# Expert stage of a hybrid decoder block: down products in float32, norm factors on ScalarE, their product on VectorE

## The chip, the cores and the metric

The kernel runs on one core of a Trainium2 chip. A core has TensorE (matrix products, with a row of its own for weight loads), VectorE, ScalarE, GpSimd (POOL below) and SyncE (SP), which issues most DMAs; each engine takes its instructions in order. The metric is the device time in microseconds (us), as the median of three runs.

## What is computed

A decoder block for 2048 tokens of 1024 channels: an attention and pooling mixer, then a mixture of 32 experts of which each token takes two, then a final norm. The change touches the experts:

```python
def expert_block(args):
    xb, e = args
    return (jax.nn.silu(xb @ w_gate[e]) * (xb @ w_up[e])) @ w_down[e]

y_rows = lax.map(expert_block, (x_blocks, block_e)).reshape(R, D)
y_rows = y_rows * row_w[:, None].astype(y_rows.dtype)
out = jnp.zeros((T + 1, D), y_rows.dtype).at[row_token].add(y_rows)[:T]
...
return rmsnorm(x, norm_f_g)
```

All arrays are float32; `w_gate` and `w_up` are 1024 x 256 for each expert, `w_down` 256 x 1024.

## The kernel before

The mixer (four blocks of 512 tokens) comes first and ends with the routing, which writes tables of rows for each expert. Then the expert stage goes through 16 pairs of experts. An expert has 128 row slots; a pair has 56 more that its experts share (`RW`, `CAP`).

A product of float32 values is made of three products in f16 (`PASSES`): a value is split into a high half, its rounding to f16, and a low half, the rest. ScalarE writes the high half of a weight piece of 128x1024 (`msplit`, line 1170), VectorE the low half (line 1171). Weights are scaled by 64, which `DSC` takes out again.

The steps of a pair stand in `PLAN`, in the order in which they are handed to a scheduler, which then sets each engine's order by costs of its own:

- S: SP loads weight pieces (`mst` for gate and up, `msd` for down, 512 KB each, 12 a pair), and `msplit` splits those of the next pair into `mwh`.
- U (`mo_up`, line 1263): gate and up products of both experts, 192 matmuls of 184 columns.
- A (`mo_act`): sigmoid on ScalarE, two products on VectorE (lines 1272 and 1273) into `sg`, then the high half of the activations on ScalarE (line 1276) and the low half on POOL (line 1277), both in `ac`.
- X (`mo_x`): rows of the next pair, transposed by TensorE (line 1208; line 1221 for the shared ones, by selection products with `sel`), copied from PSUM to `xT` by ScalarE and VectorE (lines 1227 and 1229).
- R and B: gathers of rows (`mh`, line 1194) and of the sums so far (`mx`, line 1246), indirect DMAs that POOL issues.
- D (`mo_out`, line 1293): for each of the two experts two halves of 512 columns, 24 matmuls in all, which VectorE adds to `mx` (line 1296). For the shared rows (`mo_rest`, line 1306) 24 more, with either half of the columns on half of the array's columns, two at a time.
- F (`finish`): the square sum of a row on ScalarE (line 1337), its scaling on VectorE (1342), the power -0.5 on POOL (1343), times a flag on VectorE (1316). The norm factors y = gain x r + flag are made on VectorE (lines 1318 and 1322), the product of y and the sums on POOL (line 1323), and POOL stores it by an indirect DMA (line 1251).

The loads of the sums of a pair wait until the stores of the pair two before it have landed. Behind the last pair come two loops for rows past the capacity, which run zero times here.

## Time and profile before

| | |
|---|---|
| runs | 1747.66, 1753.17, 1753.48 us; median 1753.17 |
| span of the profiled execution, first to last instruction | 1743.5 us |
| the profiled execution's own time | not recorded apart; the runs lie 4 to 10 us above the span |
| TensorE busy | 1531.6 us (88%) |
| VectorE busy | 1231.3 us (71%) |
| POOL busy | 813.0 us (47%) |
| ScalarE busy | 706.3 us (41%) |
| mean granted clock of TensorE | 0.946 |

The granted clock is the share of TensorE's full clock (2.4 GHz) that it was given, between one half and one. A busy share over the whole span mixes stages with different limits, so a stage is read through windows of its own. The ends of matmuls are modelled, and records in a row overlap; the time from one start to the next tells what a matmul costs.

### The profile page before, as it was taken

What the parts mean: (1) busy time and instruction counts of PE and PEld (TensorE: products, weight loads), DVE (VectorE), ACT (ScalarE), POOL (GpSimd) and SP (SyncE); (2) the same over time, 40 slices, a digit from 0 to 9 for tenths busy, and PEclk for the clock granted to TensorE, in tenths of its full rate; (3) what the DMA queues carried; (4) which work ended last, traced back from release to release, by engine and by line L of the source; (5) the groups of instructions that cost most, each with busy time, mean ns of one, the idle gap of its engine ahead of it and who ended that gap; (6) DMA issues with size and microseconds to landing.
All of it is one profiled execution on the core that took longest, in us unless ns stands there. A gap on an engine that the chain in (4) does not pass through costs nothing.

```text
span 1743.5 us, 28315 instructions
## 1 busy us (share of the span) xinstructions
PE 1531.6 (88%) x10777; PEld 930.4 (53%) x10777; DVE 1231.3 (71%) x1941; ACT 706.3 (41%) x1089; POOL 813.0 (47%) x620
## 2 busy tenths in 40 slices
PE   6888989979999899999799999967897888888784
PEld 3364434447544347644347744446675676666563
DVE  7678886799737357736247743368898999998984
ACT  5633464533324231223230211234664565565541
POOL 1446453556324113423223401215777777777764
PEclk9999999989999999999999999977999899998997
DMA  7444689976859895658787557669688878878722
GB/s 251 133 128 156 218 251 245 285 235 248 268 164 220 274 326 195 187 161 223 193 262 227 163 167 206 172 227 333 222 299 281 295 258 302 305 260 285 264 89 77
DMA packets 244812, 394.70 MB, mean 226 GB/s; under 512 B 154507, under 2 KB 157963, under 8 KB 244672
## 3 DMA queue, kind: packets, MB, share of 16 engines
q1 hardware_dynamic: 222144, 324.50, 60.1%
q0 software_dynamic: 22528, 68.35, 10.7%
q8 instruction: 86, 1.41, 0.3%
q14 instruction: 54, 0.44, 0.1%
HBM read 294.03 MB, written 75.50 MB: 212 GB/s over the span
## 4 chain that ended last, share of the span: by engine, by line
PE 33%; issue 16%; DVE 14%; POOL 14%; DMA 9%; ACT 2%; SPq 1%; POOLq 0%; DVEq 0%; ACTq 0%
PE aux L321 6%; PE acc L321 5%; PE acc L751 5%; PE acc L504 4%; PE acc L736 4%; DMA bt<-bt 3%; DVE mwh L1171 2%; DVE w L173 2%; POOL y L1323 2%; PE acc L1293 2%; POOL out_dram L1251 2%; POOL mx L1246 2%; PE acc L1263 2%; DMA out_dram<-x 2%; DMA w<-in_wv_dram 2%
## 5 line engine op out<-in xcount | busy, mean ns | idle before, releaser
L1263 PE MATMUL acc<-xT,mwh 128*128 128x184 f16 x3072 | 247.6, 243 | 0.0
L1263 PEld LDWEIGHTS <-mwh 128*128 128x128 f16 x3072 | 243.8, 98 | 6.4 <-issue 6.3
L173 DVE SCALAR_TENSOR_TENSOR w<-w 128x1024 f16<-128x1024 f32 x110 | 158.2, 1445 | 93.4 <-ACT w L172 93.1
L1171 DVE SCALAR_TENSOR_TENSOR mwh<-mst,mwh 128x1024 f16<-128x1024 f32 x128 | 194.8, 1539 | 1.7 <-ACT mwh L1170 1.0
L751 PE MATMUL acc<-w,bt 128*128 128x512 f16 x768 | 171.5, 385 | 16.2 <-DMA bt<-bt 15.6
L736 PE MATMUL acc<-w,bt 128*128 128x512 f16 x768 | 170.9, 382 | 9.2 <-DVE et L330 6.5
L321 PEld LDWEIGHTS <-hS 128*128 128x128 f16 x1056 | 104.1, 100 | 135.4 <-issue 18.5
L172 ACT ACTIVATE w<-w 128x1024 f16<-128x1024 f32 x110 | 112.2, 1028 | 154.7 <-DMA w<-in_wv_dram 61.6
L1293 PE MATMUL acc<-mwh,ac 128*128 128x512 f16 x384 | 113.4, 445 | 54.2 <-POOL ac L1277 42.3
L1170 ACT ACTIVATE mwh<-mst 128x1024 f16<-128x1024 f32 x128 | 128.7, 1047 | 30.6 <-PE acc L1263 23.1
L1323 POOL TENSOR_TENSOR y<-mx,y 128x1024 f32<-128x1024 f32 (+1 forms) x45 | 112.5, 2500 | 51.6 <-DVE y L1318 37.7
L321 PE MATMUL aux<-w,hS 128*128 128x512 f16 x528 | 130.1, 397 | 6.5 <-ACT et L336 4.4
L751 PEld LDWEIGHTS <-bt 128*128 128x128 f16 x768 | 75.3, 99 | 111.5 <-DMA bt<-bt 17.1
L736 PEld LDWEIGHTS <-bt 128*128 128x128 f16 x768 | 75.2, 98 | 103.1 <-issue 13.8
L504 PEld LDWEIGHTS <-w 128*128 128x128 f16 x1176 | 112.1, 99 | 32.2 <-issue 7.1
L321 PEld LDWEIGHTS <-hT 128*128 128x128 f16 x792 | 77.2, 98 | 94.1 <-issue 2.7
L321 PE MATMUL acc<-w,hS 128*128 128x512 f16 x528 | 120.8, 379 | 1.6 <-DVE w L173 1.6
L741 POOL TENSOR_TENSOR et<-et 128x512 f32<-128x512 f32 x32 | 41.4, 1296 | 164.0 <-DVE et L739 164.0
L666 ACT ACTIVATE bt<-et 128x512 f16<-128x512 f32 x48 | 30.2, 629 | 196.2 <-POOL et L741 116.4
L330 DVE SCALAR_TENSOR_TENSOR et<-aux,et 128x512 f32<-128x512 f32 x99 | 65.7, 681 | 45.8 <-PE aux L321 45.8
L1293 PEld LDWEIGHTS <-ac 128*128 128x128 f16 x384 | 38.9, 111 | 110.3 <-POOL ac L1277 48.8
L380 POOL TENSOR_TENSOR w<-w 128x1024 f32<-128x1024 f32 x24 | 62.6, 2614 | 72.3 <-DVE w L173 29.7
(291 smaller groups left out, 2869.2 us busy)
## 6 DMA issues: line engine op xcount, KB each, us to landing
w<-wkeep SPq DMA_DIRECT2D x168, 512.0 KB, 4.7
mst<-in_we_dram SPq DMA_DIRECT2D x128, 512.0 KB, 6.8
wkeep<-w SPq DMA_DIRECT2D x70, 512.0 KB, 3.1
w<-in_wv_dram SPq DMA_DIRECT2D x64, 512.0 KB, 5.2
msd<-in_we_dram SPq DMA_DIRECT2D x64, 512.0 KB, 5.5
x<-in_x_dram SPq DMA_DIRECT2D x32, 512.0 KB, 5.3
w<-in_wm_dram SPq DMA_DIRECT2D x16, 512.0 KB, 4.9
out_dram<-x POOLq DMA_DIRECT2D x16, 512.0 KB, 6.4
```

The source lines that it names most:

```text
L172: nc.scalar.activation(w[:, 0, c:], f[:, c:], AF.Copy, scale=WSC)
L173: nc.vector.scalar_tensor_tensor(w[:, 1, c:], f[:, c:], WSC, w[:, 0, c:], op0=OP.mult, op1=OP.subtract)
L321: nc.tensor.matmul(p, L[name](i, c, k), w[k // 2][:, a, (k % 2) * 512:(k % 2 + 1) * 512], start=k == 0 and m == 0, stop=k == 3 and m == 2)
L330: nc.vector.scalar_tensor_tensor(o[i], ps[i], DSC, x[i], op0=OP.mult, op1=OP.add)
L504: nc.tensor.matmul(ps[:, :h], w[:, i, k * 128:(k + 1) * 128], L[name](c, k), start=k == 0 and m == 0, stop=k == 3 and m == 2)
L736: nc.tensor.matmul(ps, lhs, w[k // 2][:, a, (k % 2) * 512:(k % 2 + 1) * 512], start=k == 0 and i == 0, stop=k == 3 and i == 2)
L751: nc.tensor.matmul(ps, self.mT[t][k // 4][:, 4 * c + k % 4], w[hf][k // 2][:, a, (k % 2) * 512:(k % 2 + 1) * 512], start=k == 0 and i == 0 ...
L1170: nc.scalar.activation(w[:, 0], f, AF.Copy, scale=WSC)
L1171: nc.vector.scalar_tensor_tensor(w[:, 1], f, WSC, w[:, 0], op0=OP.mult, op1=OP.subtract)
L1263: nc.tensor.matmul(ps[:, c * CAP:(c + 1) * CAP], self.part(W[o], a, col, 128), xT[:, b, k], start=k == 0 and i == 0, stop=k == KT - 1 and ...
L1293: nc.tensor.matmul(ps, s["ac"][i][:, b, f, :128], self.part(s["W"][3 * i + 2], a, f * D + hf * 512, 512), start=f == 0 and n == 0, stop=f ...
L1323: (nc.vector if s["P"] == 15 else nc.gpsimd).tensor_tensor(y, x, y, op=OP.mult)
```

## The change

The down weights stay in float32 as they arrive: no split, no `mwh` for them, and 8 buffers `msd` instead of 4. The activations stay in float32 in `sg` (4 buffers instead of 2). The down products multiply these directly, one matmul instead of three. The scale of 16 x 64 in the weights of the rows goes. The norm factors move from VectorE to ScalarE, their product with the sums from POOL to VectorE. Comments and docstrings go too, so that the lines shift.

```diff
-        V.tensor_scalar(w, T[:, 1], DSC, None, op0=OP.mult)
+        V.tensor_copy(w, T[:, 1])
...
-        s["W"][i] = [self.msplit(f, self.mq if i % 3 == 2 else self.mw) for f in s["F"][i]]
+        s["W"][i] = s["F"][i] if i % 3 == 2 else [self.msplit(f, self.mw) for f in s["F"][i]]
...
-    BST, BSD = 8192 // PW, 4096 // PW
+    BST, BSD = 8192 // PW, 8192 // PW
...
-        sg = mp.tile([128, 2 * CAP], F32, name="sg", bufs=2)
+        sg = mp.tile([128, 2 * CAP], F32, name="sg", bufs=4)
         nc.scalar.activation(sg, pg, AF.Sigmoid, scale=DSC)
         nc.vector.scalar_tensor_tensor(sg, pg, DSC, sg, op0=OP.mult, op1=OP.mult)
-        nc.vector.scalar_tensor_tensor(sg, pu, DSC * ASC, sg, op0=OP.mult, op1=OP.mult)
-        ac = mp.tile([128, 2, 2, CAP], F16, name="ac", bufs=2)
-        sg3 = sg.rearrange("p (c t) -> p c t", c=2)
-        nc.scalar.activation(ac[:, 0], sg3, AF.Copy)
-        nc.gpsimd.tensor_tensor(ac[:, 1], sg3, ac[:, 0], op=OP.subtract)
-        s["ac"][h] = ac
+        nc.vector.scalar_tensor_tensor(sg, pu, DSC, sg, op0=OP.mult, op1=OP.mult)
+        s["ac"][h] = sg.rearrange("p (c t) -> p c t", c=2)
...
             for f in range(2):
-                for n, (a, b) in enumerate(self.PASSES):
-                    nc.tensor.matmul(ps, s["ac"][i][:, b, f, :128], self.part(s["W"][3 * i + 2], a, f * D + hf * 512, 512),
-                                     start=f == 0 and n == 0, stop=f == 1 and n == 2)
+                nc.tensor.matmul(ps, s["ac"][i][:, f, :128], self.part(s["W"][3 * i + 2], f * D + hf * 512, 512),
+                                 start=f == 0, stop=f == 1)
...
-        m = [(h, f, n) for h in range(2) for f in range(2) for n in range(3)]
-        for q, (h, f, n) in enumerate(m):
-            a, b = self.PASSES[n]
+        m = [(h, f) for h in range(2) for f in range(2)]
+        for q, (h, f) in enumerate(m):
             for hf in range(2):
-                nc.tensor.matmul(ps[hf * 64:(hf + 1) * 64], s["ac"][h][:, b, f, CAP - 64:],
-                                 self.part(s["W"][3 * h + 2], a, f * D + hf * 512, 512),
+                nc.tensor.matmul(ps[hf * 64:(hf + 1) * 64], s["ac"][h][:, f, CAP - 64:],
+                                 self.part(s["W"][3 * h + 2], f * D + hf * 512, 512),
                                  start=q == 0, stop=q == len(m) - 1, tile_position=(0, hf * 64))
...
         if i < 2:
-            nc.vector.tensor_scalar(y, self.gf, r, nl, op0=OP.mult, op1=OP.add)
+            nc.scalar.activation(y, self.gf, AF.Identity, bias=nl, scale=r)
         else:
             for h in range(2):
                 p = slice(h * 64, h * 64 + 64)
-                nc.vector.tensor_scalar(y[p], self.gf[p, h * 512:(h + 1) * 512], r[p], nl[p], op0=OP.mult, op1=OP.add)
-        (nc.vector if s["P"] == 15 else nc.gpsimd).tensor_tensor(y, x, y, op=OP.mult)
+                nc.scalar.activation(y[p], self.gf[p, h * 512:(h + 1) * 512], AF.Identity, bias=nl[p], scale=r[p])
+        nc.vector.tensor_tensor(y, x, y, op=OP.mult)
```

The scheduler makes new orders of it. Up to the routing the four compute engines issue the same rows. Two places in the middle of the expert stage follow, with the buffer numbers as they are.

ScalarE, one pair, before (`mwh` are splits, `sg` the sigmoid, `ac` the activations' high half, `y,fss` the square sum, `xT` the copies from PSUM):

```order
L1337 ACTIVATE y,fss<-mx_10459 128x1024
L1170 ACTIVATE mwh<-msd 128x1024 x4
L1337 ACTIVATE y,fss<-mx_10460 128x1024
L1170 ACTIVATE mwh<-mst 128x1024 x2
L1271 ACTIVATE sg<-acc 128x368
L1170 ACTIVATE mwh<-mst 128x1024 x2
L1276 ACTIVATE ac<-sg 128x368
L1337 ACTIVATE y,fss<-mx_10461 128x512
L1170 ACTIVATE mwh<-mst 128x1024 x2
L1271 ACTIVATE sg<-acc 128x368
L1170 ACTIVATE mwh<-mst 128x1024 x2
L1227 ACTIVATE xT<-auxh 128x8x128
```

The same stretch of ScalarE after the change:

```order
L1170 ACTIVATE mwh<-mst 128x1024 x2
L1228 ACTIVATE xT<-auxh 128x8x128 x2
L1332 ACTIVATE y,fss<-mx_10459 128x1024
L1313 ACTIVATE y<-gfr,tlm,frs 128x1024
L1228 ACTIVATE xT<-aux 128x4x2x56 x2
L1332 ACTIVATE y,fss<-mx_10460 128x1024
L1228 ACTIVATE xT<-auxh 128x8x128
L1332 ACTIVATE y,fss<-mx_10461 128x512
L1313 ACTIVATE y<-gfr,tlm,frs 128x1024
L1170 ACTIVATE mwh<-mst 128x1024 x2
L1272 ACTIVATE sg<-acc 128x368
L1317 ACTIVATE y<-gfr,tlr,frs 64x512 x2
```

The splits of down pieces and the copies to `ac` are gone; the norm factors (`y<-gfr`) stand behind the square sums and ahead of the copies `xT` of the shared rows (`xT<-aux`).

POOL, before (`frs` is the power, `y<-mx` the product y, `out_dram<-y` a store, `mx<-out_dram` a load of sums, `mh<-h2d` a row gather):

```order
L1343 TENSOR_TENSOR frs<-frs,mhalf 128x1
L1323 TENSOR_TENSOR y<-mx_10462,y 128x1024
L1343 TENSOR_TENSOR frs<-frs,mhalf 128x1
L1246 DMA mx_10459<-out_dram,tim 128x1024
L1246 DMA mx_10460<-out_dram,tim 128x1024
L1246 DMA mx_10461<-out_dram,tih 128x512
L1251 DMA out_dram<-y,tim 2048x1024
L1323 TENSOR_TENSOR y<-mx_10463,y 128x1024
L1251 DMA out_dram<-y,tim 2048x1024
L1343 TENSOR_TENSOR frs<-frs,mhalf 128x1
L1277 TENSOR_TENSOR ac<-sg,ac 128x368
L1323 TENSOR_TENSOR y<-mx_10464,y 128x512
```

POOL after the change:

```order
L1252 DMA out_dram<-y,tih 4096x512
L1247 DMA mx_10462<-out_dram,tim 128x1024
L1247 DMA mx_10463<-out_dram,tim 128x1024
L1247 DMA mx_10464<-out_dram,tih 128x512
L1195 DMA mh_10467<-h2d,tim 128x2048
L1195 DMA mh_10465<-h2d,tim 128x2048
L1338 TENSOR_TENSOR frs<-frs,mhalf 128x1
L1195 DMA mh_10468<-h2d,tir 64x2048
L1252 DMA out_dram<-y,tim 2048x1024
L1338 TENSOR_TENSOR frs<-frs,mhalf 128x1 x2
L1252 DMA out_dram<-y,tim 2048x1024
L1252 DMA out_dram<-y,tih 4096x512
```

The tensor products between the DMAs are gone, but for the power; three loads of sums and two row gathers now stand in a row, straight ahead of the first power of a pair.

## Rows read from the trace of the kernel before

**Rows 1.** Windows (engine busy, instructions, granted clock, DMA share, GB/s): three pairs, stage, rest.

```profile
core 0: us, PE busy (x) PEld busy (x) DVE busy (x) ACT busy (x) POOL busy (x), PEclk, DMA share, GB/s
...
1192.05:1222.72 30.67, 29.86 (x312) 24.63 (x311) 27.60 (x51) 20.70 (x27) 13.68 (x12) 0.92 1.00 390
...
1362.02:1395.31 33.29, 28.16 (x291) 22.36 (x289) 31.79 (x41) 19.16 (x27) 26.95 (x17) 0.90 0.84 293
...
1494.27:1525.87 31.60, 26.55 (x290) 21.65 (x289) 30.62 (x42) 19.04 (x27) 23.36 (x17) 1.00 0.85 297
...
1192.05:1709.40 517.35, 441.77 (x4529) 348.92 (x4529) 468.16 (x618) 288.56 (x393) 374.96 (x251) 0.93 0.76 265
1709.40:1743.50 34.10, 10.09 (x52) 3.86 (x49) 11.59 (x23) 4.04 (x9) 10.22 (x11) 0.69 0.17 68
```

**Rows 2.** Timeline (start us, us, engine, line) of TensorE from 1358.

```profile
1358.32 1.06 PE L1208 MATMUL auxh<-identh,mh 128*128 128x128 f16 x16
1359.31 2.78 PE L1306 MATMUL acc<-mwh,ac 128*64 128x512 f16 x24
1362.02 15.37 PE L1263 MATMUL acc<-xT,mwh 128*128 128x184 f16 x192
1377.33 0.96 PE L1221 MATMUL aux<-sel,mh 64*128 64x112 f16 x16
```

**Rows 3.** Waits (engine line <- waited for: us, times, longest) from 1260 to 1720.

```profile
PE acc L1293 <- POOL ac L1277: 38.5, 18, 5.0
```

**Rows 4.** Line 435 (ns min/median/max), timelines of TensorE at 858 and 101.

```profile
L435 PEld LDWEIGHTS aux<-bt,wau x16: 190/190/190, 51.9 to 859.5; 128*128 128x128 f32 x16
L435 PE MATMUL aux<-bt,wau x16: 592/592/592, 52.1 to 859.9; 128*128 128x512 f32 x16
...
858.62 1.88 PE L435 MATMUL aux<-bt,wau 128*128 128x512 f32 x4
...
860.34 5.99 PE L751 MATMUL acc<-w,bt 128*128 128x512 f16 x27
...
101.68 0.66 PE L628 MATMUL aux<-et 128*64 128x128 f32 x8
102.27 0.94 PE L504 MATMUL acc<-hT,w 128*128 128x256 f16 x7
```

**Rows 5.** Line 1171 (ns); groups (busy us, mean ns) of VectorE, ScalarE, POOL, 1260 to 1720.

```profile
L1171 DVE SCALAR_TENSOR_TENSOR mwh<-mst,mwh x128: 1206/1217/4824, 1124.1 to 1689.6; 128x1024 f16<-128x1024 f32 x128
...
L1171 DVE SCALAR_TENSOR_TENSOR mwh<-msd,mwh 128x1024 f16<-128x1024 f32 x51 | 75.7, 1513 | 1.2 <-ACT mwh L1170 1.0
...
L1318 DVE TENSOR_SCALAR y<-gfr,frs,tlm 128x1024 f32<-128x1024 f32 x28 | 23.1, 825 | 0.3
L1322 DVE TENSOR_SCALAR y<-gfr,frs,tlr 64x512 f32<-64x512 f32 x28 | 20.9, 747 | 0.4
...
L1170 ACT ACTIVATE mwh<-msd 128x1024 f16<-128x1024 f32 x49 | 47.8, 1043 | 12.6 <-PE acc L1306 12.6
L1337 ACT ACTIVATE y<-mx 128x1024 f32<-128x1024 f32 x28 | 29.5, 1053 | 48.0 <-DVE mx L1296 43.1 <-issue 1.7 <-DMA mh<-h2d,tir 1.5
...
L1323 POOL TENSOR_TENSOR y<-mx,y 128x1024 f32<-128x1024 f32 x27 | 84.4, 3126 | 34.9 <-DVE y L1318 32.6 <-DVE frs L1316 2.0
...
L1277 POOL TENSOR_TENSOR ac<-sg,ac 128x368 f16<-128x368 f32 x28 | 27.8, 994 | 0.5 <-ACT ac L1276 0.2
```

**Rows 6.** Timeline behind the last up products, from 1716.

```profile
1716.33 0.75 DVE L1296 SCALAR_TENSOR_TENSOR mx<-acc,twm,mx 128x512 f32<-128x512 f32 x1 [0.93 <-PE acc L1293]
...
1718.74 0.57 POOL L1343 TENSOR_TENSOR frs<-frs,mhalf 128x1 f32<-128x1 f32 x1 [4.41 <-DVE frs L1342]
...
1719.59 0.15 DVE L1316 TENSOR_TENSOR frs<-frs,tlm 128x1 f32<-128x1 f32 x1
...
1720.62 1.23 DVE L1323 TENSOR_TENSOR y<-mx,y 128x1024 f32<-128x1024 f32 x1
```

**Rows 7.** POOL's loads of sums (busy us, mean ns); issues of stores (us to landing).

```profile
L1246 POOL DMA_INDIRECT mx<-out_dram,tim x28 | 42.9, 1531 | 9.0 <-issue 6.6 <-DMA out_dram<-y,tih 1.8 <-PE acc L1263 0.6
...
out_dram<-y,tim POOLq DMA_INDIRECT x32, 7.0
```

More of the change, by code (lines that the diff above doesn't have):

```diff
@@ L1174, in part @@
     @staticmethod
-    def part(w, a, c, n):
-        return w[c // PW][:, a, c % PW:c % PW + n]
-    BST, BSD = 8192 // PW, 4096 // PW
+    def part(w, c, n, a=None):
+        q = slice(c % PW, c % PW + n)
+        return w[c // PW][:, q] if a is None else w[c // PW][:, a, q]
+    BST, BSD = 8192 // PW, 8192 // PW
     def rows(self, s, i):
@@ L1262, in mo_up @@
                         col = k * 256 + c * 128
-                        nc.tensor.matmul(ps[:, c * CAP:(c + 1) * CAP], self.part(W[o], a, col, 128), xT[:, b, k],
+                        nc.tensor.matmul(ps[:, c * CAP:(c + 1) * CAP], self.part(W[o], col, 128, a), xT[:, b, k],
                                          start=k == 0 and i == 0, stop=k == KT - 1 and i == 2)
@@ L1388, in overflow @@
                                 skip_runtime_bounds_check_because="a count of at most 31")
-            W = [[self.msplit(self.load(self.A["we"][bass.ds(er, 1), :, c:c + PW].rearrange("o p c -> p (o c)"), i == 2), self.mq if i == 2 else self.mw)
+            W = [[self.load(self.A["we"][bass.ds(er, 1), :, c:c + PW].rearrange("o p c -> p (o c)"), i == 2)
                   for c in range(i * 2048, (i + 1) * 2048, PW)] for i in range(3)]
+            W = [[self.msplit(f, self.mw) for f in w] if i < 2 else w for i, w in enumerate(W)]
             x = self.mxs[0]
```

## The prediction

> **What bounds the kernel now.** Everything that the change touches lies in the expert stage: up to the routing the four compute engines issue the same rows before and after, so I read only that stage, and first its table of windows, cut at the first matmul of the up products of a pair [rows 1]. From the first up product to the end of the last one are 517.35 us, that is 15 whole pairs and one set of up products of 15.4 us [rows 2]: (517.35 - 15.4) / 15 = 33.5 us a pair. In the pair from 1362 VectorE is busy for 31.79 of 33.29 us, TensorE for 28.16 at a mean granted clock of 0.90, POOL for 26.95, ScalarE for 19.16. TensorE has no wait inside the up products; it loses its time behind them, in the down products, where the waits [rows 3] show 38.5 us, 18 times, on POOL's low half of the activations alone. POOL is late because its order is full of products y and indirect DMAs, and it gets its input late because the gate's two products queue on VectorE behind weight splits. So the pair is set by VectorE and POOL together, and TensorE pays. What it could do shows in the pair from 1494: clock 1.00, busy 26.55 us in 31.60.
>
> **The change, part by part.**
>
> *TensorE.* A float32 matmul of 512 columns appears in the trace at line 435: the program has 8 of them (two in each of four blocks), the trace 16 records, so each is two records [rows 4]. Four records, two matmuls, start at 858.62 and the next matmul starts at 860.34: 1.72 us, 0.86 us each, at granted clock 1.00. The f16 matmuls right behind take 5.99 us for 27, 0.22 each. Three f16 passes of 0.22 become one float32 product of 0.86: 0.2 us more. A pair has 8 such products for its two experts: 8 x 0.86 = 6.9 us for 24 x 0.217 = 5.2. The shared rows run as two products at a time on either half of the columns: 24 f16 in 2.71 us (1359.31 to 1362.02), 0.52 of what 24 x 0.217 would take [rows 2]. For float32 the only case is line 628, with 128 columns: 8 records from 101.68 to 102.27, 0.59 us, where one by one at line 435's rate they would take 8 x 128 / 512 x 0.43 = 0.86 [rows 4]. So the halves overlap in float32 too, at 0.69 of the serial time. Bounds for the 8 new products: 8 x 0.86 = 6.9 us with no overlap, 3.6 with the f16 factor of 0.52, and 4.7 with 0.69. I take 3.6, as line 628 has short matmuls that its weight loads hold up, and these have 512 columns as the f16 ones. TensorE's pair at full clock: 26.55 + (6.9 - 5.2) + (3.6 - 2.7) = **29.1 us**; with the other ends 30.2 or 32.4.
>
> Float32 weight loads take 190 ns each [rows 4]. In the four records at line 435 they fit inside the 430 ns between starts, so I cost them at nothing; the cover is the matmul before, and without it 32 loads of 0.19 are 6 us a pair (rival E). The Trainium skill (TensorE: Matmul & The Clock Gate, section Weight-path perf modes) speaks against this change here: it says that the fast way of loading weights is off for float32.
>
> The Trainium skill (Perfetto Trace Analysis, section Engine Utilization) gives half the matmul rate for one kind of float32 product; by it a product would be 0.43 us and TensorE's pair about 24 us. Line 435 shows 0.86, so the sum stands on that.
>
> *VectorE.* The groups' stretch, 1260 to 1720, holds 14 pairs (28 full norm factors). Gone are four low halves of down weights (75.7 us for 51, 4 x 1.48 = 5.9 us a pair) and the norm factors ((23.1 + 20.9) / 14 = 3.1 us) [rows 5]. Added are the products y: 1.23 us alone on VectorE [rows 6], two a pair and one of half the columns, some 0.7 us: 3.1. Net -5.9 us. Besides, a split takes 1.22 us in the median and 1.51 in the mean of the down pieces, and up to 4.8 [rows 5]. The long ones stand where POOL is busy too. POOL loses its tensor products but for the small power, so 8 x 0.3 = 2.4 us a pair of the splits that stay may go as well; nothing, if it is the indirect DMAs that stretch them. VectorE's pair: 31.8 - 5.9 - 2.4 = 23.5 us, at worst 26. It is no longer the bound.
>
> *ScalarE.* Four high halves of down weights (4 x 1.04 us [rows 5]) and two smaller copies of the activations go. The norm factors come, two a pair and two of half the columns, which the trace of before has not on this engine. Nearest is the square of the same tile, 1.05 us [rows 5]. That is the lower bound; twice that is the upper, since a factor also reads a scale and a bias per row. I take 1.1, as the length follows the columns in all rows of this engine: 2 x 1.1 + 2 x 0.6 = 3.4, net below zero. Even at twice that ScalarE stays under 23 us of 29, and the work is hidden.
>
> *POOL.* Products y and the low half of the activations go: (84.4 + 27.8) / 14 = 8 us a pair [rows 5] and the half-width product besides; some 18 us remain.
>
> *DMA.* The bytes stay. A pair moves 33.29 us x 293 GB/s = 9.75 MB at a busy share of 0.84, that is 28 us of DMA time; the first pair moved 390 GB/s at a share of 1.00, at which 9.75 MB take 25 us [rows 1]. Both ends lie under 29.1, the upper one barely. Down pieces now wait in 8 float32 buffers, two pairs' worth, and each is released by the last product of the shared rows; the next load for it has a whole pair.
>
> **What is late next.** Behind the up products nothing of the down path waits for POOL any more: the activation of the first expert is ready in mid up products, that of the second has up to 24 transposes (1.0 us for 16 [rows 2]) and the first expert's 3.4 us as cover. What can hold TensorE is the new chain through the norm. In ScalarE's new order the norm factor of the first expert stands ahead of the copies xT of the shared rows, which the next up products read. Undisturbed, from the second evacuation (1716.33) to the finished factor (1719.74) passes 3.4 us [rows 6]; the factor and two copies add 2.4. From the start of the down products: 3.4 + 0.2 + 3.4 + 2.4 = 9.4 us, against 6.9 + 0.9 (the selection products of the shared rows [rows 2]) + 3.6 = 11.4 of TensorE's own work until the next up products. But VectorE has two splits and two copies to finish ahead of the evacuation, which takes 1 to 2 us, so the slack is nearly used. I put 0.6 us a pair on it.
>
> **Sum.** 29.1 + 0.6 = 29.7 us a pair instead of 33.5: 15 x 3.8 = 57 us. Behind the last up products 34.1 us pass to the end [rows 1]; there the down products take 2.6 more, the 2 us wait for POOL and the f16 copies go, and the late start of the activation (VectorE stood under POOL's products) goes: about -3. The start of the stage hangs on routing and row gathers: 0, give or take 3. Together -60. The span is 1743.5 us; the runs shown lie 4 to 10 us above it, the median 9.7, and I keep that difference: 1753.2 - 60 = **1693 us**.
>
> **The rivals.**
>
> A. *Transfers become the bound.* For it: the share is already 0.84, and of the pairs in mid stage none shown moves more than 297 GB/s. If that is all that row-wise transfers among weight loads give, 9.6 MB take 32.3 us, and 15 x 1.2 + 3 = 21 us are won: 1732. Against it: the first pair moved 390 GB/s, and loads in mid stage wait for buffers.
>
> B. *POOL's queue holds the power, and with it the next up products: slower than before.* In its new order three loads of sums and two row gathers stand straight ahead of the first power of a pair; the loads wait until the stores of the pair before have landed. They are five, 5 x 1.5 = 7.5 us by the loads' row, and a store lands 7.0 us after its issue [rows 7]. In the new order the last product y stands behind the gate's products of the first expert, some 10 us into the up products. Then the power can start at 10 + 7 + 7.5 = 24.5 us; it is needed at 15.4 + 2 + 3.4 + 0.2 + 2.4 = 23.4 (the last from 1716.33 to 1718.74 [rows 6]). Each us later lengthens the pair by one, and 5 us later the pair is longer than 33.5. That takes a last product y at 15 us and more, or slower landings. At 35 us a pair: +23 - 3, 1773. Against it: POOL has 18 us of work in 29.7.
>
> C. *The halves of the shared rows don't overlap in float32.* 32.4 + 0.6 = 33.0: -10, 1743. Against it: line 628.
>
> D. *A float32 product costs half of line 435's.* TensorE's pair falls to 24 and transfers set 28: 15 x 5.5 + 3 = 85 us, 1668. The row is against it. The Trainium skill's page above (Perfetto Trace Analysis) stands for it.
>
> E. *Float32 weight loads are not covered.* 29.7 + 6 = 35.7 us a pair: +33 - 3, 1783. Against it: the four records at line 435.
>
> That the change does not do what it says I leave out: in the new order there are 8 product rows without hi and lo, and no split of a down piece.
>
> **How the numbers follow.** My forecast 0.67 (1676 to 1713: pairs of 28.6, a little under the sum, to 31.0, with 4.7 us for the shared rows), A 0.13, B 0.06, C 0.06, D 0.04, E 0.02, others 0.02. The range takes in the forecast and A: **1672 to 1733**, leaving out 0.20. A measurement of this kernel can tell about 0.5%, 9 us, from no change: below 1744 lie the forecast, A, D and half of C, 0.87; within, the other half and the others, 0.05; above 1762 B and E, 0.08.
>
> **What would show it.** Right: up products start every 29 to 30.5 us; no wait of a down product on POOL; float32 records 0.43 us apart, shared rows in 3.6 us; splits near 1.22 us; granted clock near 1.00 through the stage; VectorE 23 to 26 us a pair. Wrong: shared rows at 6 us or more (C); TensorE waiting at the first up products for xT, with ScalarE waiting for VectorE and that for POOL's power (B); splits waiting for weight pieces at a share near 1.00 (A).

## The result and the profile after

The changed kernel takes 1673.23 us (median of 4 runs, 1667.12 to 1677.7), the kernel before beside it 1750.41 us (4 runs, 1746.97 to 1753.48): ratio 0.9565, 95% interval 0.9543 to 0.9587, 77 us less. The forecast was 1693 us in a range from 1672 to 1733: the time lies inside it by 1 us.

The page of the changed kernel, first the busy times (us, share of the span, instructions), then the chain of work that ended last by engine:

```profile
PE 1541.1 (92%) x10521; PEld 929.9 (56%) x10521; DVE 1086.1 (65%) x1858; ACT 694.1 (41%) x1057; POOL 602.9 (36%) x543
...
PE 63%; DVE 9%; issue 6%; DMA 6%; POOL 3%; ACT 1%; SPq 1%; DVEq 0%; POOLq 0%; ACTq 0%
```

The windows of the expert stage, which answer to [rows 1]: the first pair, three pairs in the middle, the stage from the first to the end of the last up product, and what lies behind it:

```profile
core 0: us, PE busy (x) PEld busy (x) DVE busy (x) ACT busy (x) POOL busy (x), PEclk, DMA share, GB/s
1191.40:1226.09 34.69, 32.66 (x291) 25.46 (x290) 23.72 (x46) 16.00 (x20) 10.35 (x11) 0.91 0.73 246
1226.09:1254.37 28.28, 28.28 (x267) 21.36 (x265) 21.02 (x35) 18.46 (x24) 11.68 (x12) 1.00 0.96 335
...
1397.76:1426.04 28.28, 28.28 (x267) 21.36 (x265) 21.11 (x35) 18.35 (x24) 13.18 (x13) 1.00 0.95 327
1512.21:1540.49 28.28, 28.28 (x268) 21.36 (x265) 21.20 (x35) 18.45 (x24) 12.15 (x13) 1.00 0.94 330
...
1191.40:1641.41 450.01, 447.98 (x4283) 345.31 (x4282) 329.36 (x543) 277.22 (x363) 174.59 (x178) 0.99 0.87 304
1641.41:1673.40 31.99, 10.65 (x35) 3.94 (x32) 8.56 (x18) 6.90 (x10) 4.73 (x6) 0.71 0.09 36
```

TensorE is busy without a break in every pair but the first, at granted clock 1.00. VectorE fell from 31.79 to 21.1 us a pair, POOL from 26.95 to some 12. The first pair is long (34.69 us): TensorE stands twice for 1 us among its up products, until 1196.1 and 1197.5, waiting for nothing that the profile shows, the clock over the pair is 0.91, and 24 records more stand in it. In the profile of the same kernel's second measurement (below) the first pair takes 31.08 us, at a clock of 0.94 and without these waits, so part of its length varies from run to run. The other 14 pairs follow at 28.28 and 28.95 us by turns, (1626.20 - 1226.09) / 14 = 28.58 us in the mean. The timeline of TensorE (start us, us, line) over one of them answers to [rows 2, 4]:

```profile
1397.76 15.36 PE L1264 MATMUL acc<-xT,mwh 128*128 128x184 f16 x192
1412.96 1.50 PE L1209 MATMUL auxh<-identh,mh 128*128 128x128 f16 x24
1414.40 0.37 PE L1222 MATMUL aux<-sel,mh 64*128 64x112 f16 x4
1414.70 7.13 PE L1289 MATMUL acc<-msd,sg 128*128 128x512 f32 x16
1421.76 0.76 PE L1222 MATMUL aux<-sel,mh 64*128 64x112 f16 x12
1422.45 3.65 PE L1301 MATMUL acc<-msd,sg 128*64 128x512 f32 x16
```

Nothing stands between one row and the next. The experts' eight float32 products take 7.06 us to the start of the next row, the shared rows 3.6, for 5.2 and 2.7 before.

Its waits (engine line <- waited for: us, times, longest), of all engines from 1226 to 1626, then of TensorE alone over the whole stage:

```profile
POOL mx L1247 <- DMA out_dram<-y,tih: 70.4, 14, 6.9
POOL frs L1338 <- DVE frs L1337: 68.9, 28, 7.7
ACT mwh L1170 <- PE acc L1264: 49.2, 35, 1.9
...
PE acc L1264 <- issue: 2.0, 2, 1.0
```

The 38.5 us of [rows 3] are gone. The other engines now wait a lot, POOL for stores that must land (5 us a pair) and ScalarE for TensorE, and none of that reaches TensorE, whose only idle time is the 2 us in the first pair. Its groups (busy us, mean ns, idle before), which answer to [rows 5] and the loads of [rows 7], from 1226 to 1626:

```profile
L1171 DVE SCALAR_TENSOR_TENSOR mwh<-mst,mwh 128x1024 f16<-128x1024 f32 x112 | 134.2, 1219 | 18.0 <-ACT mwh L1170 17.4 <-issue 0.6
...
L1313 ACT ACTIVATE y<-gfr,tlm,frs 128x1024 f32<-128x1024 f32 x28 | 34.6, 1236 | 19.7 <-DVE frs L1311 19.7
...
L1247 POOL DMA_INDIRECT mx<-out_dram,tim x28 | 33.9, 1209 | 74.7 <-DMA out_dram<-y,tih 70.4 <-issue 4.3
L1338 POOL TENSOR_TENSOR frs<-frs,mhalf 128x1 f32<-128x1 f32 x42 | 23.6, 562 | 69.2 <-DVE frs L1337 68.9
L1317 ACT ACTIVATE y<-gfr,tlr,frs 64x512 f32<-64x512 f32 x28 | 22.5, 805 | 0.2
```

**Where the 70 us of the span came from.** Start of the stage 1192.05 to 1191.40: -0.65. Its 15 pairs: 517.35 - 15.4 = 502.0 us before, 34.69 + 14 x 28.58 = 434.8 after: -67.1. The last set of up products 15.4 to 15.2: -0.2. Behind it 34.10 to 31.99: -2.1. Sum -70.1, as the spans say (1743.5 to 1673.4).

The stage's two rows also tell what kind of time went; this is an estimate, as the clock is given to two places. Before, TensorE was idle for 517.35 - 441.77 = 75.6 us and busy for 441.77 at a clock of 0.93, which is 410.8 us of work at the full clock. After, it was idle for 2 us and busy for 447.98 at 0.99, 443.5 us of work. So 74 us of waits and some 26 us of lower clock went, and some 33 us of longer products came.

### The profile page after: what moved, and what is told of

Read it like the earlier page. It is cut to its first block, busy times and chain, and to the rows that moved or that the text cites. A ratio compares the mean times of both kernels' runs of the same rounds, so it can differ in the third digit from the quotient of the medians.

```text
span 1673.4 us, 27526 instructions
## 1 busy us (share of the span) xinstructions
PE 1541.1 (92%) x10521; PEld 929.9 (56%) x10521; DVE 1086.1 (65%) x1858; ACT 694.1 (41%) x1057; POOL 602.9 (36%) x543
## 4 chain that ended last, share of the span: by engine, by line
PE 63%; DVE 9%; issue 6%; DMA 6%; POOL 3%; ACT 1%; SPq 1%; DVEq 0%; POOLq 0%; ACTq 0%
PE acc L1264 15%; PE acc L751 7%; PE aux L321 7%; PE acc L1289 7%; PE acc L321 6%; PE acc L736 6%; PE acc L504 5%; DMA bt<-bt 3%; PE acc L1301 3%; DVE w L173 2%; PE auxh L1209 2%; DVE et L330 1%; DMA w<-in_wv_dram 1%; SPq L243 1%; PE aux L1222 1%
## 5 line engine op out<-in xcount | busy, mean ns | idle before, releaser
L751 PE MATMUL acc<-w,bt 128*128 128x512 f16 x768 | 171.8, 385 | 15.4 <-DMA bt<-bt 15.4
L1171 DVE SCALAR_TENSOR_TENSOR mwh<-mst,mwh 128x1024 f16<-128x1024 f32 x128 | 153.2, 1219 | 19.6 <-ACT mwh L1170 19.0
L321 PE MATMUL aux<-w,hS 128*128 128x512 f16 x528 | 126.6, 389 | 6.8 <-ACT et L336 3.6
L1289 PE MATMUL acc<-msd,sg 128*128 128x512 f32 x256 | 113.7, 597 | 0.0
L321 PE MATMUL acc<-w,hT 128*128 128x512 f16 x396 | 93.0, 381 | 4.3 <-DVE w L173 4.0
L321 PE MATMUL aux<-w,hT 128*128 128x512 f16 x396 | 91.5, 379 | 0.0
L330 DVE SCALAR_TENSOR_TENSOR et<-acc,et 128x512 f32<-128x512 f32 x99 | 65.8, 683 | 37.3 <-PE acc L321 37.3
```

The source lines that it names most:

```text
L321: nc.tensor.matmul(p, L[name](i, c, k), w[k // 2][:, a, (k % 2) * 512:(k % 2 + 1) * 512], start=k == 0 and m == 0, stop=k == 3 and m == 2)
L330: nc.vector.scalar_tensor_tensor(o[i], ps[i], DSC, x[i], op0=OP.mult, op1=OP.add)
L751: nc.tensor.matmul(ps, self.mT[t][k // 4][:, 4 * c + k % 4], w[hf][k // 2][:, a, (k % 2) * 512:(k % 2 + 1) * 512], start=k == 0 and i == 0 ...
L1171: nc.vector.scalar_tensor_tensor(w[:, 1], f, WSC, w[:, 0], op0=OP.mult, op1=OP.subtract)
L1289: nc.tensor.matmul(ps, s["ac"][i][:, f, :128], self.part(s["W"][3 * i + 2], f * D + hf * 512, 512), start=f == 0, stop=f == 1)
```

## The experiments

The theory was: VectorE and POOL were late together and TensorE paid; the change unloads both, and then TensorE's own work sets the pair. Its rivals said that one half of the change does it all and the other costs, that transfers or the norm's chain become the bound, or that the wait in the rows was itself the price. Lengths of pairs below leave out the first pair of the stage.

### Either half of the change alone

The kernel before with the norm part alone:

```diff
-            nc.vector.tensor_scalar(y, self.gf, r, nl, op0=OP.mult, op1=OP.add)
+            nc.scalar.activation(y, self.gf, AF.Identity, bias=nl, scale=r)
...
-        (nc.vector if s["P"] == 15 else nc.gpsimd).tensor_tensor(y, x, y, op=OP.mult)
+        nc.vector.tensor_tensor(y, x, y, op=OP.mult)
```

> The kernel before with one part of the change: norm factors on ScalarE, their product with the sums on VectorE. Down products stay three f16 passes with split weights. Theory (TensorE waited for queues on POOL and VectorE; without those waits its own work sets the pair): TensorE's own pair with f16 passes is 28.6 - 10.6 + 7.9 = 25.9 us; VectorE has 21.2 + 4 x 1.22 = 26.1 us and POOL's low half of the activations as the only long tensor work, so a pair takes 28 to 30.5 us and the run about 1670 to 1705. Rival (the down splits on VectorE are what counts, the norm part is hidden): VectorE stays near 31 us a pair and the run near 1735 to 1750.

Measured: 1685.24 us, ratio 0.9629 (0.9599 to 0.9659). The pairs vary from 26.3 to 35.8 us, 29.5 in the mean.

The changed kernel with the norm part undone, that is the float32 down products alone:

```diff
-            nc.scalar.activation(y, self.gf, AF.Identity, bias=nl, scale=r)
+            nc.vector.tensor_scalar(y, self.gf, r, nl, op0=OP.mult, op1=OP.add)
...
-        nc.vector.tensor_tensor(y, x, y, op=OP.mult)
+        (nc.vector if s["P"] == 15 else nc.gpsimd).tensor_tensor(y, x, y, op=OP.mult)
```

> The change without its norm part: down products in float32, norm factors on VectorE and their product on POOL as before. Theory: VectorE has 21 us of work, some 2.5 more for splits that POOL's products stretch from 1.22 to about 1.5 us, POOL about 22; both lie under TensorE's 28.6, so the pair stays at 28.6 to 29.5 and the run at 1673 to 1690: the norm part alone would be worth 0 to 15 us on top of the float32 products. Rival (POOL's products y hold stores, loads of sums and the power, and with them the next up products): pairs of 31 us and more, 1710 and up, with TensorE waiting at the first up products or at down products.

Measured: 1676.16 us, ratio 0.9563 (0.954 to 0.9587): the same as the whole change within the intervals. The pairs take 28.73 us. So the norm part brings 65 us alone and nothing that the intervals could tell on top of the other half; the float32 products bring 75 us alone, of the 77 of both. The two gains are not parts of a sum: the products alone unload VectorE and POOL as far as TensorE needs (it has no wait in these pairs), the norm part alone nearly so, and what one has freed the other cannot free again. The windows show the difference that is left, in 100 us of the norm part alone and then, from the other kernel, of the products alone (columns as above):

```profile
1355.00:1455.00 100.00, 92.97 (x992) 73.00 (x991) 92.94 (x138) 80.47 (x106) 60.23 (x48) 1.00 0.94 340
```

```profile
1355.00:1455.00 100.00, 100.00 (x901) 72.33 (x898) 86.49 (x125) 50.03 (x69) 69.16 (x53) 1.00 0.96 337
```

With float16 down products VectorE is still at 93 in 100 and TensorE still waits for it and for POOL (14.8 us on POOL's low half over the whole stage); with float32 ones VectorE has 13 in 100 to spare, enough, although POOL's products y are back and stretch what VectorE does. In the second kernel even operations on one element per row last 2 us under them:

```profile
L1171 DVE SCALAR_TENSOR_TENSOR mwh<-mst,mwh 128x1024 f16<-128x1024 f32 x112 | 144.3, 1317 | 0.3 <-ACT mwh L1170 0.3
L1318 POOL TENSOR_TENSOR y<-mx,y 128x1024 f32<-128x1024 f32 (+1 forms) x42 | 84.2, 2004 | 11.8 <-DVE y L1317 7.6 <-ACT mwh L1170 2.4 <-DVE y L1313 1.1
...
L1336 DVE TENSOR_TENSOR fss<-fss,frs 128x1 f32<-128x1 f32 x14 | 28.6, 2041 | 0.5
```

### VectorE or POOL: the norm part and the wait, piece by piece

The kernel before with the products y on VectorE, nothing else:

```diff
-        (nc.vector if s["P"] == 15 else nc.gpsimd).tensor_tensor(y, x, y, op=OP.mult)
+        nc.vector.tensor_tensor(y, x, y, op=OP.mult)
```

> The kernel before with one edit: the products y of the norm go from POOL to VectorE in all pairs (the factors stay on VectorE, the down products in float16). The theory that POOL's queue is what TensorE waits for, and that its products stretch VectorE's work: POOL loses (84.4 + half-width products) some 7 us a pair, VectorE gains 3.1 us for them and loses some 2 us of stretch, so VectorE stays near 32 us a pair and is the bound: pairs of 31 to 33 us, 1715 to 1745 us. A rival (POOL alone counts): as with the factors on ScalarE, too, some 29.5 us a pair and 1685 us. Another rival (VectorE's added 3.1 us decide): pairs of 34 us or more, no gain or a loss, 1750 us or more.

Measured: 1708.55 us, ratio 0.9777 (0.9751 to 0.9802), pairs of 31.2 us in the mean. The time is a little under the first theory's range: VectorE got no busier although 3 us of work came to it (29.1 us a pair for 30.7 before).

The kernel before with the factors on ScalarE, nothing else:

```diff
-            nc.vector.tensor_scalar(y, self.gf, r, nl, op0=OP.mult, op1=OP.add)
+            nc.scalar.activation(y, self.gf, AF.Identity, bias=nl, scale=r)
...
```

> The kernel before with one edit: the norm factors go from VectorE to ScalarE (the products y stay on POOL, the down products in float16). With the products y alone moved to VectorE the time fell by 39 us, with both moved by 65. If the two edits add up (VectorE and POOL are each late by turns), this one is worth the rest, some 26 us: VectorE loses 3.1 us of 31.8 a pair, ScalarE gains 3.7 and has room: 1724 us (1714 to 1734), pairs of 31.5 to 32.5 us. A rival (POOL's queue alone counts, and it keeps its products and its order): 1742 us or more, and waits on POOL's low half of 30 us or more in the stage. Another rival (VectorE's load alone counts): as both edits, 1690 us or less.

Measured: 1731.3 us, ratio 0.9872 (0.9845 to 0.9899), pairs of 32.4 us. By the ratios this is 22 us, the products y alone 39, both 65: the two nearly add up, and neither engine alone decides. The busy times of these traces say the same (VectorE, POOL and the pair, us, in the mean): 30.7, 24.9 and 33.7 before; 29.1, 17.8 and 31.2 with the products y moved; 27.3, 23.6 and 32.4 with the factors moved; 26.4, 17.2 and 29.5 with both. The pair with the factors moved is longer than that with the products y moved although VectorE has less to do, so VectorE's load alone does not set it. With both moved it is 1.7 us shorter than with the products y alone although POOL has nearly as much to do, so POOL's load alone does not either. Why the products y are worth more than they weigh, the splits show: first with the products y on VectorE, then with them left on POOL (1230 to 1600):

```profile
L1171 DVE SCALAR_TENSOR_TENSOR mwh<-mst,mwh 128x1024 f16<-128x1024 f32 x96 | 116.9, 1233 | 0.2
L1171 DVE SCALAR_TENSOR_TENSOR mwh<-msd,mwh 128x1024 f16<-128x1024 f32 x46 | 54.9, 1219 | 6.0 <-ACT mwh L1170 6.0
```

```profile
L1171 DVE SCALAR_TENSOR_TENSOR mwh<-mst,mwh 128x1024 f16<-128x1024 f32 x90 | 125.5, 1415 | 4.3 <-ACT mwh L1170 3.9
L1171 DVE SCALAR_TENSOR_TENSOR mwh<-msd,mwh 128x1024 f16<-128x1024 f32 x48 | 70.3, 1500 | 5.0 <-ACT mwh L1170 5.0
```

A split lasts 1.22 to 1.23 us without products y on POOL and 1.42 to 1.50 with them, while POOL issues its indirect DMAs in both. So it is POOL's products y that stretch VectorE's work, and not its indirect DMAs, which the prediction had left open. The Trainium skill (SBUF — State Buffer, section Who interferes with whom) says this: a VectorE instruction with two inputs from SBUF contends with a POOL instruction that reads SBUF, and one of them waits until the other is done. The runs agree: splits and the one-element sum have two such inputs. Two inputs are not the whole condition here: `sel<-identh,own` (L1215), with one input tensor and one value per row, takes 0.25 us in the mean in the changed kernel and 1.6 with the products y back on POOL.

Last, the kernel before without the very work that TensorE waited for in [rows 3] on POOL:

```diff
-        nc.gpsimd.tensor_tensor(ac[:, 1], sg3, ac[:, 0], op=OP.subtract)
+        nc.vector.tensor_tensor(ac[:, 1], sg3, ac[:, 0], op=OP.subtract)
```

> The kernel before with one word changed: the low half of the activations on VectorE instead of POOL, so that the only work that TensorE waited for in its rows (38.5 us on POOL's low half) leaves POOL; norm, factors, products y and the float16 down products stay. The theory (VectorE and POOL set the pair together, the wait on POOL only shows where they are late): POOL loses 2 x 0.95 us a pair, VectorE gains 2 x 0.55 on 31.8 us, with its splits still stretched by the products y on POOL; TensorE then waits for VectorE instead, and the time stays within 15 us of before: 1738 to 1758 us, pairs of 33 us. A rival (the wait in the rows is the price): 38 us less or more, 1713 us or less, pairs of 31 us.

Measured: 1727.86 us, ratio 0.9897 (0.9868 to 0.9927): 18 us. That is more than the theory's 15 and half of what the rival said: both ranges were missed. TensorE's waits of the stage (1190 to 1720), before and in this kernel:

```profile
PE acc L1293 <- POOL ac L1277: 42.3, 21, 5.0
PE acc L1293 <- ACT ac L1276: 10.3, 5, 3.6
PE auxh L1208 <- DVE xT L1229: 10.1, 6, 3.6
```

```profile
PE auxh L1208 <- DVE xT L1229: 20.0, 8, 3.4
PE acc L1293 <- ACT ac L1276: 17.5, 7, 4.2
PE acc L1293 <- DVE ac L1277: 13.1, 8, 3.2
PE acc L1306 <- DVE mx L1296: 6.0, 5, 2.3
```

42.3 us on POOL go, and the waits on VectorE and ScalarE grow. All rows of this view add up to 82 us before and 63 after, 19 less. The wait that a profile names is not the price of removing it.

### Is the pair TensorE's work and nothing else?

The changed kernel with half as many down products (each half of the columns takes one of the two blocks of 128 hidden channels, so half of each sum is left out; the shared rows' products are halved in the same way):

```diff
-            for f in range(2):
-                nc.tensor.matmul(ps, s["ac"][i][:, f, :128], self.part(s["W"][3 * i + 2], f * D + hf * 512, 512),
-                                 start=f == 0, stop=f == 1)
+            f = hf
+            nc.tensor.matmul(ps, s["ac"][i][:, f, :128], self.part(s["W"][3 * i + 2], f * D + hf * 512, 512),
+                             start=True, stop=True)
...
```

> The changed kernel with half of the down products: of the two rows of 128 hidden channels each half of the output columns takes one, so 4 float32 products for the experts and 4 for the shared rows in place of 8 and 8; that half of the sum is left out. Theory (TensorE alone sets 28.6 us a pair, next come the transfers): TensorE falls to 28.6 - 3.5 - 1.8 = 23.3 us; the transfers, 9.4 MB a pair, take 24.5 to 27 us, so the pair is 25 to 27 and the run 1673 - 15 x 2.6 = about 1634 (1618 to 1650). If another engine's chain (the norm through POOL and ScalarE) already stood close behind TensorE, the pair stays at 28 and more: 1660 and up. If transfers and all else have room, 23.3: 1595.

Measured: 1621.16 us, ratio 0.9254 (0.9232 to 0.9277), pairs of 25.4 us. A window of it:

```profile
1255.00:1355.00 100.00, 96.75 (x1039) 79.39 (x1037) 84.49 (x141) 71.41 (x96) 52.08 (x47) 1.00 1.00 380
```

Less TensorE work gives shorter pairs at once, and the next limit is in sight: the DMA share is 1.00 at 380 GB/s, so transfers need about 25 us a pair, 3 under TensorE's 28.6. That they alone set these pairs is not shown: TensorE's waits in this stage are named as VectorE's, the longest in sum 9.8 us for the adding of its products to `mx`.

The other way, more TensorE time with the same work: the shared rows' products all on one half of the columns, then all on the other.

```diff
-        for q, (h, f) in enumerate(m):
-            for hf in range(2):
+        for hf in range(2):
+            for q, (h, f) in enumerate(m):
```

> The changed kernel with the shared rows' eight float32 products in another order: all four on the first half of the columns, then all four on the second, instead of one on either half in turn. The theory (two products overlap only where they lie on different halves of the columns and follow each other, and the pair is TensorE's work and nothing else): the 16 records take 16 x 0.43 = 6.9 us, less one product's worth at the change of halves at most, instead of 3.6; pairs of 28.6 + 2.9 to 3.3 = 31.5 to 31.9 us, and 15 or 16 times that, 1673 + 44 to 52 = 1717 to 1725 us. A rival (the products' length does not depend on their order): 3.6 us and 1673 us. Another rival (TensorE has slack behind the down products which swallows the surplus): 6.9 us, but pairs that are less than 2 us longer, 1700 us or less.

Measured: 1701.16 us, ratio 0.9739 (0.9716 to 0.9763), 28 us over the changed kernel; pairs of 30.35 us. The timeline of one pair's shared rows:

```profile
1252.21 5.42 PE L1301 MATMUL acc<-msd,sg 128*64 128x512 f32 x16
```

5.42 us where 6.0 to 6.9 were expected and 3.6 stand in the changed kernel. The pair grew by 30.35 - 28.58 = 1.8 us, as the products did (5.42 - 3.6): no slack behind the down products, the theory holds and the second rival falls. The size was off, since the halves overlap even in this order, which the scheduler keeps: read in steps of 0.1 us, four records start 0.43 apart alone, then two at a time, and the last four alone again, 12 steps of 0.43 us. The trace doesn't say which record belongs to which half; as read here, the second half starts with the first half's fifth record, long before its eighth.

The changed kernel with four buffers for down weights, as before, instead of eight:

```diff
-    BST, BSD = 8192 // PW, 8192 // PW
+    BST, BSD = 8192 // PW, 4096 // PW
```

> The changed kernel with 4 buffers for the down pieces instead of 8. Theory: the next pair's 4 pieces are then loaded after the last product of the shared rows, 16.6 us before they are needed, and take some 7 us; TensorE does not wait, the pair stays at 28.6 and the run within 0.5% of 1673. Rival (the second set of buffers carries part of the gain, as these loads stand ahead of gate and up pieces in SP's queue): the splits come late, the pair is 30 us and more, 1695 and up.

Measured: 1677.55 us, ratio 0.9577 (0.9547 to 0.9606), pairs of 28.6 us: no difference from the changed kernel that the intervals could tell.

### A mix of both kinds of product

If TensorE sets the pair, its own work is what is left to save. The changed kernel with the second expert's down product in three float16 passes again:

```diff
...
-        s["W"][i] = s["F"][i] if i % 3 == 2 else [self.msplit(f, self.mw) for f in s["F"][i]]
+        s["W"][i] = s["F"][i] if i == 2 else [self.msplit(f, self.mq if i == 5 else self.mw) for f in s["F"][i]]
...
+        if h == 0:
+            nc.vector.scalar_tensor_tensor(sg, pu, DSC * ASC * WSC, sg, op0=OP.mult, op1=OP.mult)
+            s["ac"][h] = sg3
+            return
+        nc.vector.scalar_tensor_tensor(sg, pu, DSC * ASC, sg, op0=OP.mult, op1=OP.mult)
+        ac = mp.tile([128, 2, 2, CAP], F16, name="ac", bufs=2)
+        nc.scalar.activation(ac[:, 0], sg3, AF.Copy)
+        nc.gpsimd.tensor_tensor(ac[:, 1], sg3, ac[:, 0], op=OP.subtract)
+        s["ac"][h] = ac
...
```

> The changed kernel with the down product of the second expert of each pair taken back to three float16 passes (its down weights split into hi and lo again, its activations into hi and lo with the low half on POOL); the first expert's stays in float32. The theory (TensorE's own work alone sets the pair now, and half of the float32 products costs half of their surplus): the surplus is 8 x 0.2 = 1.7 us for the experts' products and 0.9 us for the shared rows, so half of it, 1.3 us, goes: 28.6 - 1.3 = 27.3 us a pair, VectorE some 23.5 us a pair (two splits of 1.22 us come back), no wait of a down product on POOL's low half worth more than 0.3 us a pair, since POOL keeps no product y and the second expert's activations have 24 transposes and the first expert's products as cover. 15 x 1.3 = 20 us: some 1654 us (1646 to 1664). A rival (POOL's low half or the transfers, at a busy share of 0.95 already, give the wait back): pairs of 28.3 us or more, 1669 us or more, with waits of the second expert's products on POOL, or of splits on weight pieces.

> The changed kernel once more, word for word, as the measure for the runs beside it: 1667 to 1678 us, pairs of 28.6 us.

Measured: the mix 1673.49 us, ratio 0.9575 (0.9552 to 0.9598); the changed kernel beside it 1671.55 us, ratio 0.9574 (0.9554 to 0.9595). No gain: the rival's number, but not its pairs. From the fifth on the pairs are 27.4 to 28.2 us long, as the theory said; the four before them take 34.2, 28.1, 31.8 and 28.4. In the first of these TensorE waits 3.99 us for POOL, in the third 2.4 us, and the clock over these two pairs is 0.90 and 0.95. POOL's timeline in the first shows why:

```profile
1239.94 1.04 POOL L1252 DMA_INDIRECT out_dram<-y,tih  x1 [2.94 <-DVE y L1329]
1246.35 2.07 POOL L1247 DMA_INDIRECT mx<-out_dram,tim  x1 [5.36 <-DMA out_dram<-y,tih]
1248.72 1.01 POOL L1247 DMA_INDIRECT mx<-out_dram,tim  x1 [0.31 <-issue]
1250.04 1.01 POOL L1247 DMA_INDIRECT mx<-out_dram,tih  x1 [0.30 <-issue]
1251.36 1.00 POOL L1195 DMA_INDIRECT mh<-h2d,tim  x1 [0.30 <-issue]
1252.66 1.00 POOL L1195 DMA_INDIRECT mh<-h2d,tim  x1 [0.30 <-issue]
1253.68 0.90 POOL L1282 TENSOR_TENSOR ac<-sg,ac 128x368 f16<-128x368 f32 x1
```

The low half needs 0.9 us and nothing of what stands ahead of it; but three loads of sums wait until the last store has landed, two row gathers follow, and POOL takes its work in order. That is rival B's mechanism with another victim. So the low half went to VectorE, which has the room:

```diff
-        nc.gpsimd.tensor_tensor(ac[:, 1], sg3, ac[:, 0], op=OP.subtract)
+        nc.vector.tensor_tensor(ac[:, 1], sg3, ac[:, 0], op=OP.subtract)
```

> The mixed kernel (first expert's down product in float32, second expert's in three float16 passes) with the low half of the second expert's activations on VectorE instead of POOL. The theory (in the mixed kernel TensorE's own work fell to 27.4 to 27.8 us a pair, as its later pairs show, and the gain was lost in the first pairs alone, where POOL held the low half behind loads of sums and row gathers that wait for the last store: 4.0 and 2.5 us of wait, and a clock of 0.96 after them): no wait of a down product on POOL, all pairs 27.4 to 27.9 us, clock 1.00, VectorE some 0.5 us a pair more, 24 us; 15 x 0.9 = 13 us under the changed kernel, 1658 us (1652 to 1664). A rival (the long first pairs come from the transfers or the start of the stage, whatever engine has the low half): a pair of 31 us or more among the first four again, 1667 us or more.

Measured: 1662.26 us, ratio 0.949 (0.9469 to 0.9511), pairs of 27.5 to 27.6 us but one of 28.56. And the other expert in float16:

```diff
-        s["W"][i] = s["F"][i] if i == 2 else [self.msplit(f, self.mq if i == 5 else self.mw) for f in s["F"][i]]
+        s["W"][i] = s["F"][i] if i == 5 else [self.msplit(f, self.mq if i == 2 else self.mw) for f in s["F"][i]]
...
-        if h == 0:
+        if h == 1:
...
```

> As the mixed kernel with the low half on VectorE, but the other way round: the first expert's down product in three float16 passes, the second expert's in float32. TensorE's work is the same; the halves of the first expert's activations have the second expert's up products as cover, and the second expert's activations need no halves, so nothing made late in the pair stands ahead of the down products but two products of the gate. The theory gives 27.4 to 27.9 us a pair and 1658 us (1652 to 1664), as the run beside it, or up to 5 us less if what is left of waits was on the second expert's halves. A rival (transfers at a busy share of 0.95 and more set the pair): 28.3 us or more, 1667 us or more.

Measured: 1657.92 us, ratio 0.9455 (0.9429 to 0.948), pairs of 27.4 us in the mean. It beats both kernels: its interval lies wholly below the changed kernel's (0.9543 to 0.9587, and 0.9554 to 0.9595 in the second measurement), some 1.2%. The window of its middle, columns as above:

```profile
1400.00:1500.00 100.00, 99.93 (x1012) 77.70 (x1012) 88.56 (x142) 73.78 (x98) 47.19 (x43) 1.00 0.96 347
```

TensorE is still the bound, with VectorE at 89 and transfers at 0.96 close behind it.

## Why the prediction was right, and where it was off

The code and the sign were right, the mechanism too; the forecast was 20 us too cautious, in sizes. The time lies under the 1676 us to which the forecast's own part of the range reached, and inside the whole range by 1 us; that much was luck, and the second measurement's 1671.55 us lies just outside.

- **What bound the kernel before.** That "the pair is set by VectorE and POOL together, and TensorE pays" is shown. Relief of either helps (39 and 22 us), the wait on POOL alone is worth 18 of its 42 us.
- **TensorE's float32 terms** were right: 7.06 us for 6.9, and 3.6 for the shared rows, where the f16 factor was taken between bounds of 3.6 and 6.9; their 16 records run two at a time. Rivals C, D and E fall with these rows: weight loads of 190 ns [rows 4] fit between the starts here too. A float32 product is four float16 passes long here, 0.86 / 0.217 = 4.0. The Trainium skill (FP8 and Floating Point Precision, section TensorE Precision Notes) says that a true float32 product makes four passes, and the trace agrees. The halved rate of the Trainium skill (Perfetto Trace Analysis, section Engine Utilization), on which rival D stood, does not hold for this product.
- **The base of TensorE's pair was 0.7 us too high.** The pair after is 28.58 us, so without its down products 28.58 - 7.06 - 3.6 = 17.9 us; the prediction's 26.55 - 5.2 - 2.7 gave 18.65. The 0.2 by which 6.9 was short take some of it back, and the pair came out 0.5 under the 29.1 of the sum. The 26.55 us were a busy time from a pair with four waits in it, and what stands before a wait shows its full modelled end: two float16 products there 0.60 us (1510.46) for 2 x 0.217. Four times 0.17 are about the 0.7 us, as an estimate.
- **The 0.6 us for the chain of the norm were not needed.** TensorE has no wait there. The undisturbed chain was right: in the tail after the change, the start of the second evacuation, the power and the finished factor (1648.29 + 0.16 - 1645.08 = 3.4 us, the prediction's figure from [rows 6]).

```profile
1645.08 0.75 DVE L1292 SCALAR_TENSOR_TENSOR mx<-acc,twm,mx 128x512 f32<-128x512 f32 x1 [0.97 <-PE acc L1289]
...
1647.69 0.57 POOL L1338 TENSOR_TENSOR frs<-frs,mhalf 128x1 f32<-128x1 f32 x1 [13.50 <-DVE frs L1337]
1648.29 0.16 DVE L1311 TENSOR_TENSOR frs<-frs,tlm 128x1 f32<-128x1 f32 x1 [0.69 <-POOL frs L1338]
```

- **Pairs in sum:** 14 pairs 1.1 us shorter than the forecast's 29.7 (-16 us) and a first pair 5 us longer, which no step had foreseen: -67 for the -57 predicted. The 28.58 us also lie under the 29 to 30.5 that were to show the forecast right. Tail -2.1 for -3, start -0.65 for 0.
- **"the runs shown lie 4 to 10 us above it, the median 9.7, and I keep that difference"** (above the span) is the step that failed for 8 of the other 10 us. The profiled run after took 1675.19 us at a span of 1673.4, 1.8 us around it, and every later profile where its own time is known (1681.97 and 1680.1, 1676.98 and 1675.2) says about the same. So the profiled execution of before took about 1745 us, a run at the low end of the scatter, and 1745.3 - 70.1 is the 1675.2 measured. The difference to the median of other runs was scatter, not time around the span: 9.7 was put where 1.8 belongs. The last 2 us are scatter too, since the profiled run after lies 2 above the median of its kernel.
- **VectorE** at 21.1 us for 23.5: splits came to 1.22 us as said, the sum of one element per row (`fss`) from 0.81 to 0.16 us, and the 31.8 us that the sum started from were those of one pair, for 30.7 in the mean. **ScalarE's factor** took 1.24 and 0.81 us for the 1.1 and 0.6 taken, inside the bounds, and hidden. **POOL** is busy for 11 to 13 us a pair, not 18: its power fell from 1.05 to 0.56 us and its loads from 1.53 us [rows 7] to 1.21.
- **Rival A** (transfers) was wrong for this kernel and is next in line: 0.95 at 28.3 us a pair, 1.00 at 25.4. **Rival B**'s wait exists (5 us a pair on landing stores) and costs nothing here; in the first mix the same queue cost all that the mix had won.

## What to carry to other kernels

When two engines are late by turns, gains of parts overlap: here two halves of a change bring 65 and 75 us alone and 77 together, so what a part is worth on top must be asked of the kernel that has the other. Cost a change by the pair of the engine that will bind next, built from its rows without stalls in them, and when it binds look at its own work: the cheaper kind of product for one of two experts, with its helper kept off a queue that waits for stores, was worth another 1.2%. Compare a predicted span with the profiled run's own time, not with the median of other runs.

## What the runs showed of the hardware

- Products y on POOL stretch VectorE's two-input work: splits of 1.22 us to 1.42 to 1.50 in the mean, sums of one element per row to 2.0 us. Moving the products y (3 us a pair on VectorE) from POOL to VectorE left VectorE no busier in sum (29.1 us a pair for 30.7) and won 39 us.
- Float32 products on the two halves of the columns overlap as f16 ones do, 16 records in 3.6 us; they overlap in part even when all of one half stand ahead of all of the other, 5.42 us.
- With half the down products, DMA in mid stage reached 380 GB/s at a share of 1.00 among row-wise transfers and weight loads, nearly the 390 of the first pair before [rows 1].
